# Scaling the attention probabilities on ScalarE, with one reciprocal and one gate product per pair of heads

## The chip, the cores and the metric

The kernel runs on one core of one Trainium2 chip. The metric is the device time of one launch in microseconds (us), as the median of several runs. The engines of the core are named as the profile names them: PE (TensorE matmul), PEld (TensorE weight load), DVE (VectorE), ACT (ScalarE), POOL (GpSimd) and SP (SyncE, which issues DMAs).

## The reference

Two layers, each on a residual stream of 512 positions by 1024 channels, all in float32:

```python
for l in range(DEPTH):                                   # DEPTH = 2
    x = x + 0.5 * swiglu_ffn(x, ffn1 ...)                # 1024 -> 2816 -> 1024
    h = rms_norm(x, mix_norm[l])
    p = h @ w_in[l]                                      # split into four groups
    y = concat[ pool_mixer(p_a), rwkv7_mixer(p_b), nsa_mixer(p_c), short_conv_mixer(p_d) ]
    x = x + y @ w_out[l]
    x = x + 0.5 * swiglu_ffn(x, ffn2 ...)
```

The change lies in the third mixer. Its four heads of 64 channels attend in three branches, and each branch's output is multiplied by a gate before the three are added:

```python
gt  = jax.nn.sigmoid(gates).reshape(B, S, H, 3)
out = gt[..., 0:1] * o_cmp + gt[..., 1:2] * o_sel + gt[..., 2:3] * o_win
# o_sel, o_win: softmax(q k^T * scale - slope * distance, causal) @ v
```

With 512 positions the selected and the window branch both reduce to full causal attention, each with keys and values of its own that all four heads share.

## The kernel before, in words

Every large product is made of three matmuls (`mm3`, lines 209 to 211): operands are cut into a high and a low part, so `hi*hi`, `lo*hi` and `hi*lo` are added in PSUM. The cut of a weight tile is a cast on ACT (line 203) and a subtraction on DVE (line 204).

A layer is a half-step FFN, the mixing stage, the output projection, and a second FFN. In the mixing stage the columns of the input projection arrive tile by tile (`tilep`), and four mixers work on them. Two of them are long chains of small operations that run side by side: the RWKV recurrence (`Rwkv.solve`, then `Rwkv.chain`, eight steps in two halves, each half followed by `Rwkv.out`), and the attention (`Net.nsa`).

The attention works through 16 units per layer: 4 query blocks `i` of 128 positions, 2 pairs of heads `j`, 2 branches `br`. For each unit, `scores(i, j, br)` computes the two heads of the pair, with `w = 128 * (i + 1)` keys:

- line 589, PE: two matmuls of queries and keys into a PSUM bank `d`;
- line 591, DVE: adds the distance bias, scales and writes the tile `s`, and leaves the row's extreme in `mx` (a short read of the accumulator follows);
- line 594, ACT: the exponential in place, with the row's sum in `sum` (again a short read of the accumulator follows);
- lines 596 and 597, DVE: the reciprocal of the sum, times the gate, in `cf`, one column per head;
- line 598, POOL: the tile `s` times `cf`, row by row.

`values` then transposes the probabilities of both heads on PE (line 616), cuts the result on ACT and DVE (lines 618 and 619), and multiplies by the values (line 623, with the compressed branch's line 627) into the PSUM bank `o`. After the second branch, lines 633 (ACT) and 634 (DVE) move the unit's output to `T`. When all units of a pair are done, `T` is cut for the output projection (lines 463 and 464).

The tiles `s` of scores and the cut transposes come out of one ring of seven buffers (`ring`, `rring`); `mx`, `sum` and `cf` have four buffers each.

What stands in which order on an engine is set by the framework's scheduler when the program is built, from the priorities in `Net.PRI` and its own costs: the recurrence has a better priority than the attention units, and these a better one than the remaining projection tiles, which fill in. Each engine then takes its instructions strictly in the order that was written down. Lines that come back in the prediction beside these: 904 and 911 or 912 (copies between the steps of the recurrence), 931 (its state update on DVE), 183 to 189 and 995 (normalisation in `Rwkv.out`), 216 (a scaled copy on ACT in the FFN), 355 (the reload of `x` after the mixers, issued from POOL).

Of the kernel before, what the change touches and what calls it, by code (L numbers as in the profile page):

```python
# [13 lines left out]
AF = mybir.ActivationFunctionType  # L14
ALU = mybir.AluOpType
# [83 lines left out]
class Net:  # L99
# [424 lines left out]
    def nsa(self, raw, L1, cmp):  # L524
        nc = self.nc
# [38 lines left out]
        gh = gt.rearrange("p (i h b) -> p i h b", h=4, b=3)  # L564
# [13 lines left out]
        def scores(i, j, br):  # L578
            w = P * (i + 1)
            out = []  # L580
            for hp in range(2):
                h = 2 * j + hp
                if hp == 0 or w > 256:
                    pq, sc, o = self.pd(), self.ring(), 0
                else:
                    o = w
                ph, sh = pq[:, o:o + w], sc[:, o:o + w]
                for k in range(2):
                    nc.tensor.matmul(ph, Q2[h][:, i * P:(i + 1) * P], K2[:, br, k, :w], start=(k == 0), stop=(k == 1))  # L589
                mx = self.small(1, "mx", bufs=4)  # L590
                nc.vector.tensor_tensor_reduce(sh, ph, c["bias"][:, S - w:S],
                                               -(2.0 ** (-2 * (h + 1))), 3.0e38, ALU.add, ALU.min, mx)
                sm = self.small(1, "sum", bufs=4)
                nc.scalar.activation(sh, sh, AF.Exp, bias=mx, scale=-1.0, accum_out=sm)
                cf = self.small(1, "cf", bufs=4)
                nc.vector.reciprocal(cf, sm)
                nc.vector.tensor_mul(cf, cf, gh[:, i, h, 1 + br:2 + br])
                nc.gpsimd.tensor_scalar(sh, sh, cf, None, ALU.mult)
                out.append(sh)
            return out  # L600

        def values(scs, i, j, br):
# [33 lines left out]
        def run():  # L636
            yt = self.mt("T16", [P, 2, S])
            self.y[4], self.y[5] = yt[:, 0], yt[:, 1]
            prev = None
            for u in units:  # L640
                sc = at(scores, *u)
                if prev is not None:
                    at(values, *prev)
                prev = (sc, *u)
                yield
            at(values, *prev)
# [578 lines left out]
```

## Time and profile before

| | |
|---|---|
| median of 3 runs | 2081.13 us (2078.3 to 2084.09) |
| the profiled execution | 2080.37 us, of which the profiled span is 2078.6 us |
| PE busy | 2026.1 us, 97% of the span |
| PEld busy | 1646.0 us, 79% |
| DVE busy | 1042.8 us, 50% |
| ACT busy | 665.3 us, 32% |
| POOL busy | 329.9 us, 16% |
| attention of layer 1, first to last line 589 | 521.8 to 627.8 us after the span's start |
| attention of layer 2, first to last line 589 | 1550.7 to 1650.1 us |

How to read it: busy time is the union of the records of an engine, and the records of overlapping matmuls run into each other, so a busy PE is not a PE at its peak. Shares over the whole span are an average over FFN stages, where PE works without a break, and mixing stages, where it waits for others. The change touches only the second kind.

### The profile page before, as it was taken

The page shows a single profiled execution, that of the slowest core. Times are in us where ns is not written, and L with a number is a line of the kernel's source. Part 1 is how long each engine was busy: PE and PEld are TensorE (multiplying, and loading weights), DVE is VectorE, ACT ScalarE, POOL GpSimd, SP SyncE. Part 2 cuts the span into 40 slices and gives each one's busy share as a digit, 9 for nine tenths or more (in the row PEclk, how much of TensorE's full clock was granted, in tenths as well). Part 3 has the DMA queues.
Part 4 walks back from the last instruction along what each step waited for, and adds up shares of the span by engine and source line. Part 5 has one row for each costly group of instructions (what it writes and reads, how often), then busy time and mean ns, then how long its engine had stood idle before and what let it go on. Part 6 is the DMA issues. An engine that isn't in the chain of part 4 may idle for free.

```text
span 2078.6 us, 25265 instructions
## 1 busy us (share of the span) xinstructions
PE 2026.1 (97%) x10132; PEld 1646.0 (79%) x10132; DVE 1042.8 (50%) x1866; ACT 665.3 (32%) x1053; POOL 329.9 (16%) x311
## 2 busy tenths in 40 slices
PE   8999999998999999999999999999988999999999
PEld 6888888876767888888888888887766778888887
DVE  5434344567676534343544343355686754334433
ACT  4322223332344322232333222233324443222221
POOL 1110111102332110011011001111033411100110
PEclk9999999998999999999999999999999999999999
DMA  5223223322302322322332232244133032223223
GB/s 198 93 90 103 101 89 124 128 102 64 71 18 91 102 89 82 114 90 89 104 102 102 84 110 100 75 133 149 68 74 77 1 102 102 95 84 116 86 92 97
DMA packets 61078, 196.76 MB, mean 95 GB/s; under 512 B 29472, under 2 KB 29600, under 8 KB 46240
## 3 DMA queue, kind: packets, MB, share of 16 engines
q1 hardware_dynamic: 58400, 186.76, 28.0%
q0 software_dynamic: 2560, 8.39, 1.1%
q8 instruction: 79, 1.29, 0.3%
q14 instruction: 39, 0.32, 0.0%
HBM read 183.58 MB, written 8.93 MB: 93 GB/s over the span
## 4 chain that ended last, share of the span: by engine, by line
PE 92%; DVE 4%; DMA 1%; issue 1%; ACT 1%; POOL 0%; SPq 0%; DVEq 0%; POOLq 0%; ACTq 0%
PE d L209 15%; PE d L210 15%; PE d L211 15%; PE r L211 8%; PE r L209 8%; PE r L210 8%; PE n L209 5%; PE n L211 5%; PE n L210 5%; PE o L623 1%; PE r L1010 1%; PE n L616 1%; PE d L589 0%; PE c L901 0%; DVE t L1032 0%
## 5 line engine op out<-in xcount | busy, mean ns | idle before, releaser
L203 ACT CAST wh<-w 128x1024 fp32r<-128x1024 f32 (+2 forms) x360 | 344.4, 957 | 1103.9 <-issue 334.5
L204 DVE TENSOR_TENSOR wl<-w,wh 128x1024 fp32r<-128x1024 f32 (+2 forms) x360 | 404.4, 1124 | 211.7 <-ACT wh L203 204.1
L209 PE MATMUL d<-hh,wh 128*128 128x512 f32 x1008 | 400.0, 397 | 6.8 <-ACT hh L216 6.8
L210 PE MATMUL d<-hl,wh 128*128 128x512 f32 x1008 | 400.6, 397 | 1.7 <-DVE hl L217 1.7
L211 PE MATMUL d<-hh,wl 128*128 128x512 f32 x1008 | 399.0, 396 | 0.0
L270 POOL TENSOR_TENSOR al<-t,ah 128x512 fp32r<-128x512 f32 x88 | 152.7, 1735 | 1062.5 <-ACT ah L269 1062.5
L210 PE MATMUL r<-hl,wh 128*128 128x512 f32 x736 | 286.8, 390 | 0.0
L211 PE MATMUL r<-hh,wl 128*128 128x512 f32 x736 | 286.5, 389 | 0.0
L209 PE MATMUL r<-hh,wh 128*128 128x512 f32 x736 | 286.5, 389 | 0.0
L209 PEld LDWEIGHTS d<-hh,wh 128*128 128x128 f32 x1008 | 192.6, 191 | 50.2 <-ACT hh L216 6.8
L210 PEld LDWEIGHTS d<-hl,wh 128*128 128x128 f32 x1008 | 192.4, 191 | 44.7 <-DVE hl L217 3.6
L211 PEld LDWEIGHTS d<-hh,wl 128*128 128x128 f32 x1008 | 192.4, 191 | 42.9 <-issue 2.0
L264 DVE TENSOR_TENSOR t<-d,rs 128x512 f32<-128x512 f32 x88 | 60.5, 691 | 266.3 <-PE d L211 260.5
L268 DVE TENSOR_TENSOR t<-t,r 128x512 f32<-128x512 f32 x88 | 60.5, 688 | 221.1 <-PE r L211 220.9
L209 PEld LDWEIGHTS r<-hh,wh 128*128 128x128 f32 x736 | 138.2, 188 | 28.7
L211 PEld LDWEIGHTS r<-hh,wl 128*128 128x128 f32 x736 | 138.2, 188 | 28.6
L210 PEld LDWEIGHTS r<-hl,wh 128*128 128x128 f32 x736 | 138.2, 188 | 28.5
L209 PE MATMUL d<-ah,wh 128*128 128x512 f32 x352 | 136.9, 389 | 0.0
L210 PE MATMUL d<-al,wh 128*128 128x512 f32 x352 | 136.9, 389 | 0.0
L211 PE MATMUL d<-ah,wl 128*128 128x512 f32 x352 | 136.9, 389 | 0.0
L209 PE MATMUL n<-ah,wh 128*128 128x512 f32 x352 | 136.9, 389 | 0.0
L210 PE MATMUL n<-al,wh 128*128 128x512 f32 x352 | 136.9, 389 | 0.0
(307 smaller groups left out, 2372.1 us busy)
## 6 DMA issues: line engine op xcount, KB each, us to landing
w<-in_g SPq DMA_DIRECT2D x87, 1024.0 KB, 4.9
w<-in_d SPq DMA_DIRECT2D x64, 704.0 KB, 4.1
w<-in_win SPq DMA_DIRECT2D x20, 1024.0 KB, 4.9
w<-in_wout SPq DMA_DIRECT2D x8, 1024.0 KB, 5.3
xd<-x POOLq DMA_DIRECT2D x16, 256.0 KB, 4.2
x<-xd POOLq DMA_DIRECT2D x16, 256.0 KB, 5.7
x<-in_x SPq DMA_DIRECT2D x8, 256.0 KB, 5.3
s<-in_cmpk SPq DMA_DIRECT2D x8, 256.0 KB, 5.9
```

The costliest lines, as they stand in the source:

```text
L203: self.nc.scalar.copy(hi, w)
L204: self.nc.vector.tensor_sub(lo, w, hi.bitcast(F32))
L209: self.nc.tensor.matmul(ps, wh[:, sl], xh[:, k], start=(first and i == 0), stop=False)
L210: self.nc.tensor.matmul(ps, wh[:, sl], xl[:, k], start=False, stop=False)
L211: self.nc.tensor.matmul(ps, wl[:, sl], xh[:, k], start=False, stop=(last and i == n - 1))
L264: nc.vector.tensor_mul(t, pg, self.rs)
L268: nc.vector.tensor_mul(th, th, pu)
L270: nc.gpsimd.tensor_sub(al, th, ah.bitcast(F32))
L616: nc.tensor.transpose(ptr[:, k * P:(k + 1) * P], scs[hp][:, b * P:(b + 1) * P], self.ident)
L623: nc.tensor.matmul(acc, VT[:, br, b], pT[k][:, o:o + 2 * P], start=(br == 0 and b == 0 and k == 0), stop=(br == 1 and b == i and k == 1))
L1010: nc.tensor.matmul(pm[:, i * P:(i + 1) * P], AK[j][hs, ch].rearrange("p a b -> p (a b)"), KR[j][hs, ch].rearrange("p a b -> p (a b)"), sta ...
```

## The change

The two heads of a unit now share one `sum` tile and one `cf` tile of two columns. The exponential of each head writes its sum into its own column. After both heads, one reciprocal and one product with the gates (two gates, strided) serve the pair, and two ACT instructions multiply the two score tiles by their column of `cf`. POOL no longer takes part in the attention units.

```diff
         def scores(i, j, br):
             w = P * (i + 1)
             out = []
+            sm = self.small(2, "sum", bufs=4)
             for hp in range(2):
...
-                sm = self.small(1, "sum", bufs=4)
-                nc.scalar.activation(sh, sh, AF.Exp, bias=mx, scale=-1.0, accum_out=sm)
-                cf = self.small(1, "cf", bufs=4)
-                nc.vector.reciprocal(cf, sm)
-                nc.vector.tensor_mul(cf, cf, gh[:, i, h, 1 + br:2 + br])
-                nc.gpsimd.tensor_scalar(sh, sh, cf, None, ALU.mult)
+                nc.scalar.activation(sh, sh, AF.Exp, bias=mx, scale=-1.0, accum_out=sm[:, hp:hp + 1])
                 out.append(sh)
+            cf = self.small(2, "cf", bufs=4)
+            nc.vector.reciprocal(cf, sm)
+            nc.vector.tensor_mul(cf, cf, gh[:, i, 2 * j:2 * j + 2, 1 + br])
+            for hp in range(2):
+                nc.scalar.activation(out[hp], out[hp], AF.Copy, scale=cf[:, hp:hp + 1])
             return out
```

In the changed program the exponential is still line 594, the reciprocal is line 597, the product line 598 and the scaling line 600; every later line is one higher. The scheduler wrote both mixing stages anew.

**First place: ACT, layer 1, the first two units with 512 keys.** Here `s` is a score tile, `n` a bank of transposes, `R` and `sav` belong to the recurrence, `T` takes a unit's output. Before:

```order
L594 ACTIVATE s_4513,sum_4518<-s_4513,mx_4516 128x512
L463 CAST yh_4240<-t_4910 128x256 x2
L594 ACTIVATE s_4525,sum_4530<-s_4525,mx_4528 128x512
L618 CAST s_4541<-n_4536 128x512
L911 COPY sav_2608<-c_4982 64x128
L618 CAST s_4552<-n_4549 128x256
L594 ACTIVATE s_4563,sum_4568<-s_4563,mx_4566 128x512
L633 COPY T_619_3930<-o_4487 64x128
L594 ACTIVATE s_4575,sum_4580<-s_4575,mx_4578 128x512
```

And in the changed program:

```order
L594 ACTIVATE s_4466,sum_4464<-s_4466,mx_4469 128x512
L619 CAST s_4489<-n_4484 128x512
L594 ACTIVATE s_4473,sum_4464<-s_4473,mx_4476 128x512
L619 CAST s_4500<-n_4497 128x256
L905 COPY R_4916<-c_4909 128x128
L634 COPY T_619_3930<-o_4439 64x128
L594 ACTIVATE s_4512,sum_4510<-s_4512,mx_4515 128x512
L594 ACTIVATE s_4519,sum_4510<-s_4519,mx_4522 128x512
L600 ACTIVATE s_4466<-s_4466,cf_4479 128x512
L600 ACTIVATE s_4473<-s_4473,cf_4479 128x512
L912 COPY sav_2608<-c_4918 64x128
L634 COPY T_619_3930<-o_4439 64x128
```

The two scalings of a unit stand behind the two exponentials of the unit after it, and a copy of the recurrence (line 912 there) stands behind the scalings.

**Second place: DVE, the coefficients of the same stretch.** Before, with four instructions for the unit's two heads:

```order
L596 RECIPROCAL cf_4570<-sum_4568 128x1
L634 TENSOR_TENSOR T_619_3930<-T_619_3930,o_4487 64x128
L596 RECIPROCAL cf_4582<-sum_4580 128x1
L597 TENSOR_TENSOR cf_4570<-cf_4570,gt_3376 128x1
L597 TENSOR_TENSOR cf_4582<-cf_4582,gt_3376 128x1
```

And in the changed program, with two for the pair:

```order
L598 TENSOR_TENSOR cf_4479<-cf_4479,gt_3376 128x2
L189 SCALAR_TENSOR_TENSOR lrs_4824<-ru_861_4827,lrs_4824 128x8
L635 TENSOR_TENSOR T_619_3930<-T_619_3930,o_4439 64x128
L996 TENSOR_TENSOR t_4812<-t_4812,lrs_4824 128x512
L597 RECIPROCAL cf_4525<-sum_4510 128x2
L598 TENSOR_TENSOR cf_4525<-cf_4525,gt_3376 128x2
L913 COPY sav_2608<-c_4918 64x128
```

The pair's reciprocal and product each appear once, and they now come after the second head's sum.

## Rows read from the trace of the kernel before

**Rows 1.** The page's first part: span, then each engine's busy time, its share of the span and its instructions.

```profile
span 2078.6 us, 25265 instructions
PE 2026.1 (97%) x10132; PEld 1646.0 (79%) x10132; DVE 1042.8 (50%) x1866; ACT 665.3 (32%) x1053; POOL 329.9 (16%) x311
```

**Rows 2.** Busy time by stretch of the mixing stages: the stretch in us from the span's start, its length, then busy us and instructions of PE, PEld, DVE, ACT and POOL, the granted TensorE clock, DMA share and GB/s. The first two lie in layer 1, the third in layer 2.

```profile
560.00:600.00 40.00, 36.63 (x270) 27.00 (x270) 24.95 (x89) 18.68 (x53) 10.83 (x11) 0.88 0.08 27
600.00:640.00 40.00, 38.71 (x294) 29.35 (x293) 33.04 (x121) 20.77 (x55) 17.30 (x12) 0.98 0.01 1
...
1590.00:1640.00 50.00, 47.04 (x405) 34.86 (x399) 36.42 (x132) 26.43 (x76) 18.39 (x16) 0.97 0.07 23
```

**Rows 3.** Timeline of POOL in layer 1's mixing stage: start and duration in us, engine, line, operation, operands, and in brackets the idle time before it and what ended it. A row with x2 holds two scalings back to back.

```profile
552.43 0.61 POOL L598 TENSOR_SCALAR s<-s,cf 128x128 f32<-128x128 f32 x1 [11.05 <-DVE cf L597]
...
565.77 0.93 POOL L598 TENSOR_SCALAR s<-s,cf 128x256 f32<-128x256 f32 x1 [7.66 <-DVE cf L597]
...
587.61 2.47 POOL L598 TENSOR_SCALAR s<-s,cf 128x384 f32<-128x384 f32 x2 [0.45 <-DVE cf L596]
596.77 1.24 POOL L598 TENSOR_SCALAR s<-s,cf 128x384 f32<-128x384 f32 x1 [6.70 <-DVE cf L596]
...
615.25 3.37 POOL L598 TENSOR_SCALAR s<-s,cf 128x512 f32<-128x512 f32 x2 [3.31 <-DVE cf L597]
621.34 3.10 POOL L598 TENSOR_SCALAR s<-s,cf 128x512 f32<-128x512 f32 x2 [2.73 <-DVE cf L597]
627.22 3.11 POOL L598 TENSOR_SCALAR s<-s,cf 128x512 f32<-128x512 f32 x2 [2.77 <-DVE cf L597]
633.22 3.11 POOL L598 TENSOR_SCALAR s<-s,cf 128x512 f32<-128x512 f32 x2 [2.90 <-ACT s L594]
648.56 3.86 POOL L355 DMA_DIRECT2D x<-xd  x7 [12.23 <-DVE yl L464]
```

**Rows 4.** Groups of ACT over the whole span, by line and shape: count, then busy us and mean ns of one, then idle time before them and what ended most of it.

```profile
L216 ACT ACTIVATE hh<-x,vec 128x512 fp32r<-128x512 f32 x48 | 34.5, 719 | 35.8 <-DVE x L309 33.7 <-DVE x L363 2.2
...
L618 ACT CAST s<-n 128x512 fp32r<-128x512 f32 x32 | 18.3, 585 | 22.5 <-PE n L616 22.3
...
L594 ACT ACTIVATION_READ_ACCUMULATOR s<-s,mx 128x1 f32 x64 | 12.0, 188 | 0.0
...
L594 ACT ACTIVATE s<-s,mx 128x512 f32<-128x512 f32 x16 | 11.6, 723 | 8.7 <-DVE mx L591 6.1 <-DVE cf L596 1.9 <-DVE cf L597 0.6
...
L594 ACT ACTIVATE s<-s,mx 128x384 f32<-128x384 f32 x16 | 9.8, 615 | 5.4 <-DVE lrs L184 2.6 <-DVE mx L591 2.3 <-DVE cf L596 0.5
...
L594 ACT ACTIVATE s<-s,mx 128x256 f32<-128x256 f32 x16 | 8.1, 509 | 6.1 <-DVE cf L597 2.9 <-DVE mx L591 2.5 <-ACT s L618 0.4
...
L594 ACT ACTIVATE s<-s,mx 128x128 f32<-128x128 f32 x16 | 6.4, 402 | 21.7 <-DVE mx L591 17.9 <-DVE cf L596 3.8
```

**Rows 5.** Timeline of ACT for one unit with 512 keys in layer 1, columns as in rows 3.

```profile
624.39 0.72 ACT L594 ACTIVATE s<-s,mx 128x512 f32<-128x512 f32 x1
625.02 0.19 ACT L594 ACTIVATION_READ_ACCUMULATOR s<-s,mx 128x1 f32 x1
626.13 0.72 ACT L594 ACTIVATE s<-s,mx 128x512 f32<-128x512 f32 x1 [0.92 <-DVE cf L596]
626.76 0.18 ACT L594 ACTIVATION_READ_ACCUMULATOR s<-s,mx 128x1 f32 x1
```

**Rows 6.** Groups of DVE over the whole span, columns as in rows 4.

```profile
L597 DVE TENSOR_TENSOR cf<-cf,gt 128x1 f32<-128x1 f32 x64 | 11.7, 186 | 1.3
...
L596 DVE RECIPROCAL cf<-sum 128x1 f32<-128x1 f32 x64 | 10.1, 158 | 9.1 <-ACT s L594 8.6
```

**Rows 7.** Two groups of DVE in the stretch 1590 to 1672 us (layer 2), columns as in rows 4.

```profile
L995 DVE TENSOR_TENSOR t<-t,lrs 128x512 f32<-128x512 f32 x2 | 1.4, 699 | 0.0
...
L188 DVE TENSOR_TENSOR ru<-ru,rh 128x8 f32<-128x8 f32 x6 | 1.0, 162 | 0.1
```

**Rows 8.** The chain of work that ended last, in the stretch 560 to 648 us: shares of the chain by engine and line.

```profile
by line: PE o L623 13.0%; PE n L616 7.2%; PE d L589 5.8%; PE c L901 5.4%; PE o L627 5.0%; DVE s L591 5.0%; PE c L898 4.7%; PE r L948 4.2%; issue 3.8%; DVE yl L464 3.4%; PE r L951 3.1%; ACT s L618 2.7%; DVE T L634 2.6%; PE r L969 2.4%; PE c 
```

**Rows 9.** The group of line 591 on DVE in the stretch 560 to 646 us, columns as in rows 4; and its accumulator read.

```profile
L591 DVE CUSTOM_DVE_ANT_0 s<-d,cst 128x384 f32<-128x384 f32 (+2 forms) x22 | 12.2, 564 | 2.0 <-PE o L623 1.9
...
L591 DVE DVE_READ_ACCUMULATOR2_ANT mx<- 128x1 f32 x22 | 1.8, 82 | 0.0
```

**Rows 10.** The same two groups in the stretch 560 to 648 us (layer 1).

```profile
L995 DVE TENSOR_TENSOR t<-t,lrs 128x512 f32<-128x512 f32 x2 | 1.6, 825 | 0.1
...
L188 DVE TENSOR_TENSOR ru<-ru,rh 128x8 f32<-128x8 f32 x6 | 1.4, 238 | 0.1
```

**Rows 11.** Timeline of DVE, the coefficients of the unit in rows 5.

```profile
625.95 0.16 DVE L596 RECIPROCAL cf<-sum 128x1 f32<-128x1 f32 x1
...
626.87 0.15 DVE L597 TENSOR_TENSOR cf<-cf,gt 128x1 f32<-128x1 f32 x1
...
627.91 0.15 DVE L596 RECIPROCAL cf<-sum 128x1 f32<-128x1 f32 x1
...
628.11 0.15 DVE L597 TENSOR_TENSOR cf<-cf,gt 128x1 f32<-128x1 f32 x1
```

## Prediction

> **What bounds the kernel now.** I read the page first, then the mixing stages by stretch, then one attention unit engine by engine, and last the chain of work that ended last. The page has PE busy for 97% of the span [rows 1], so at first sight nothing that spares VectorE or GpSimd can count. The stretches tell it otherwise. In the 40 us from 600 us on, deep in layer 1's attention, PE is busy for 38.71 us, but its weight loads for only 29.35, while VectorE is busy for 33.04 of 40 us, ScalarE for 20.77 and GpSimd for 17.30 [rows 2]. No engine is full there and all wait for each other in turn. The POOL timeline shows the pace: the pairs of scalings with 512 keys start at 615.25, 621.34, 627.22 and 633.22 us, one unit each 6.0 us [rows 3]. The stage is a loop of short dependent steps, with VectorE the fullest after PE.
>
> How much of PE's 38.71 us is real decides what can be won at all. The record of a matmul reaches past the start of the next, so the gaps of a loop are partly covered by the tail of the matmul ahead; the weight loads, one for each matmul, leave 10.65 us of these 40 free [rows 2]. If the busy figure were the truth, 1.3 us could be won here. The Trainium skill, "Perfetto Trace Analysis", section "Identifying the Most-Contended Engine", calls matmul busy time a bad metric, since matmuls are pipelined, and wants the busy share of weight loads instead; by that rule up to 10.65 us of the stretch are open, by the busy row 1.3.
>
> The executions shown: the profiled one took 2080.37 us (span 2078.6), the median of the runs is 2081.13, 0.8 above it. I make the sum as a difference and set it against the median.
>
> **The change part by part, for one layer (16 units); there are two layers.**
>
> *Scaling moves from POOL to ACT: the latency of a unit.* On POOL one scaling takes 0.61, 0.93, 1.24 and 1.57 us for 128, 256, 384 and 512 keys (half of 3.11 for the last), and two heads go one behind the other: 3.11 us for 512, 2.47 for 384 [rows 3]. On ACT the trace has no such row at SBUF-to-SBUF with a column as scale for all widths; the nearest are the exponential with a column as bias, 0.40, 0.51, 0.62 and 0.72 us, and the FFN's scaled copy at 512, 0.72, which agrees [rows 4]. Two in a row overlap by about 0.1 us: the exponential starts at 624.39, and its accumulator read at 625.02, before its 0.72 us are over [rows 5]. So a pair takes 1.34 us at 512, 1.13 at 384, 0.92 at 256 and 0.70 at 128. But the pair must wait for the second head's sum, which comes later than the first by one exponential and its 0.19 us read, less the overlap of 0.1: 0.8, 0.7, 0.6 and 0.5 us.
> - Upper bound, where POOL does both heads back to back: 3.11 - (0.8 + 1.34) = 0.97 at 512; 2.47 - (0.7 + 1.13) = 0.64; 1.86 - (0.6 + 0.92) = 0.34; 1.22 - (0.5 + 0.70) = 0.02. Four units each: 7.9 us.
> - Lower bound, where the second head is late enough for POOL to be free: 1.57 - 1.34 = 0.23; 1.24 - 1.13 = 0.11; 0.93 - 0.92 = 0.01; 0.61 - 0.70 = -0.09. Four each: 1.0 us.
>
> All four 512 pairs of layer 1 are back to back, 384 partly [rows 3], so I take four times 0.97, two times 0.64 and two times 0.11 at 384, and 0.3 for the rest: 5.7 us. Not all of it ends up in the time, for the next unit's scores run meanwhile and VectorE is 83% busy. I count half: **2.8 us**.
>
> *VectorE's small instructions.* Four become two per unit. One reciprocal (0.158 us) and one product (0.186) fewer [rows 6], 16 times: 5.5 us of VectorE. Two columns instead of one should cost the same: line 188's eight columns take 0.162 us [rows 7]. Of line 591, which stands in the same queue at the same places, 5.0% of an 88 us chain [rows 8] = 4.4 us lie on the chain, of 12.2 + 1.8 = 14.0 us busy [rows 9]: 31%. The same share of 5.5 us: **1.7 us**; between 0 and 5.5.
>
> *VectorE next to POOL.* Some small VectorE rows are stretched in layer 1 where scalings run: line 188 takes 0.238 us in place of 0.162, six times, and line 995 takes 0.825 in place of 0.699, twice [rows 7, 10], together 0.7 us; such rows stand in the recurrence's normalisation. They should fall back. I count half: **0.3 us**. The Trainium skill, "SBUF — State Buffer", section "Who interferes with whom", says that a VectorE instruction with two SBUF inputs and a GpSimd instruction that reads SBUF exclude each other, the later one waiting for the whole of the first; by that a stretch could be 1.5 us, and the term would be some twice as large, but the rows show a mean stretch of 0.08 to 0.13 us.
>
> *ScalarE gets fuller.* Eight scalings of each width, 8 x (0.40 + 0.51 + 0.62 + 0.72) = 18.0 us, less 0.1 for each of 32: 14.8 us. Its share in the 40 us stretch goes from 52% to about 70%. The casts of line 618 and the copies of the recurrence stand in the same queue, behind scalings that wait for coefficients. Nothing to some 5 us of it can surface; ScalarE was idle for 19 of the 40 us [rows 2], and its casts mostly waited for PE (22.3 of 22.5 us) [rows 4], so I take a tenth: **-1.5 us**.
>
> *Rest.* POOL's freed time is worth nothing by itself: the reload of `x` that stands behind the last scaling in its queue waited 12.23 us, for something else [rows 3]. The shared `sum` and `cf` tiles are written and read at the same points as before, four of each; no DMA is added and none is moved past another on SP.
>
> Sum: 2.8 + 1.7 + 0.3 - 1.5 = 3.3 us per layer, 6.6 in both; the tail of each stage ends with a 512 unit whose 0.97 us lie bare, of which half is counted above, so I add 0.2 per layer. 2081.1 - 7.0 = **2074.1 us**.
>
> **The rivals.**
>
> *Nothing that can be measured.* PE takes its instructions in a fixed order with projection tiles between the units, and what the units gain is lost in waits elsewhere in the loop, or the new order of both stages costs as much as the relief brings. For it: PE's 97%, and that POOL does not appear among the lines of the chain [rows 8], so its latency may be hidden as it is. Against it: the 6.0 us pace with 3.1 us of POOL in it. By the terms, with a quarter of what I expect, 1.8 us: 2079.3 us. A measurement of this kernel can tell about 0.3%, 6 us, from no change.
>
> *Twice as much.* If the pace of the loop is the unit's own latency, the whole 5.7 to 7.9 us per layer come through, with VectorE's 1.7 on top: 7.4 to 9.6 per layer, 2062 to 2066 us, say 2064. For it: back-to-back pairs at a constant pace; against it: VectorE at 83%.
>
> *Slower: ScalarE's queue.* The scaling is now an instruction at the head of an in-order queue, waiting for two VectorE instructions. In the unit at 624 us the second sum was there at 626.94 (626.76 + 0.18), the product only at 628.26 [rows 5, 11]: 1.3 us; for the first head it took from 625.2 to 627.0, 1.8 us. If ScalarE stands still for 1.5 us in each of the 11 units of the dense part, with casts and the recurrence's copies behind it, that is 16.5 us per layer; a third of it bare is 5.5, less VectorE's 1.7: 3.8 per layer, 2081.1 + 7.6 = 2088.7 us. It decides where ScalarE's idle time before line 600 passes about 12 us per layer and PE waits for line 618's casts behind it. Against it: the scheduler put two exponentials of the next unit ahead of most scalings, so the wait is mostly filled. The Trainium skill, "ScalarE: Activation LUTs", section "Rules for kernel authors", sends multiplications to VectorE and not to ScalarE; by that rule this case is the likelier one, but no row here shows the scaling on VectorE.
>
> **How the numbers follow.** The forecast (2066 to 2075) gets 0.40, the larger gain 0.12, no measurable change 0.34, slower 0.14. Faster by over 0.3% is the first two: 0.52. The range leaves out about a tenth at either end: 2062 us, where the larger gain is nearly whole, to 2087, within the slower case.
>
> **What would show it.** Right: line 598's POOL rows are gone; the ACT group of line 600 has means of 0.40 to 0.72 us; the reciprocal and the product count 32 each instead of 64, at about 0.16 us; the last unit's pace at 512 keys falls from 6.0 to about 5.4 us; the distance from the first score matmul of a layer to the first unbroken run of output-projection matmuls shrinks by 3 to 4 us; line 188 goes to 0.16 us in both layers. Wrong, if the pace stays at 6 us with VectorE less busy (then the loop hangs on something else, PE or the recurrence), or if ACT waits long before line 600 and PE before line 623 for the casts.

## The result, and the profile after

The changed kernel took 2058.7 us (median of 4 runs, 2053.1 to 2059.4), the kernel before beside it 2081.8: a ratio of 0.9889, 95% interval 0.9866 to 0.9913. A second measurement gave 2058.6 and 0.9898 (0.9880 to 0.9917). So 23 us were won where 7 were forecast, and the time lies 3 us below the low end of the range.

The page's first part, which answers to [rows 1]:

```profile
span 2057.7 us, 25078 instructions
...
PE 2012.5 (98%) x10132; PEld 1636.9 (80%) x10132; DVE 1031.3 (50%) x1802; ACT 693.5 (34%) x1117; POOL 256.4 (12%) x247
```

The same kind of groups as in [rows 4, 6, 7], on ACT and DVE in 560 to 632 us (layer 1); line 600 is the scaling, lines 597 and 598 are the pair's coefficients, and line 188 has kept its number:

```profile
L594 ACT ACTIVATE s<-s,mx 128x512 f32<-128x512 f32 x8 | 5.8, 723 | 0.2 <-DVE lrs L189 0.2
L600 ACT ACTIVATE s<-s,cf 128x512 f32<-128x512 f32 x8 | 5.3, 714 | 0.3 <-DVE cf L598 0.3
...
L600 ACT ACTIVATE s<-s,cf 128x384 f32<-128x384 f32 x8 | 4.4, 603 | 0.0
```

```profile
L597 DVE RECIPROCAL cf<-sum 128x2 f32<-128x2 f32 x11 | 1.8, 163 | 1.7 <-ACT s L594 1.5
...
L598 DVE TENSOR_TENSOR cf<-cf,gt 128x2 f32<-128x2 f32 x11 | 1.7, 158 | 0.2
...
L188 DVE TENSOR_TENSOR ru<-ru,rh 128x8 f32<-128x8 f32 x6 | 1.0, 162 | 0.1
```

Every duration came out as forecast: scalings at 0.60 and 0.71 us, a reciprocal of two columns at 0.16, and line 188 back at 0.162. That isn't where 23 us come from. The pace of the 512-key units, which was to fall from 6.0 to 5.4 us [rows 3], did not: the last two pairs of scalings start 5.95 us apart, and from the first pair's start to the fourth's it is 18.4 us, before 18.0. The timeline of ACT, line 600, 512 keys, in layer 1 (start and duration in us):

```profile
605.02 1.32 ACT L600 ACTIVATE s<-s,cf 128x512 f32<-128x512 f32 x2
606.80 1.33 ACT L600 ACTIVATE s<-s,cf 128x512 f32<-128x512 f32 x2
617.44 1.34 ACT L600 ACTIVATE s<-s,cf 128x512 f32<-128x512 f32 x2 [0.29 <-DVE cf L598]
623.39 1.34 ACT L600 ACTIVATE s<-s,cf 128x512 f32<-128x512 f32 x2
```

What did change is seen when each layer's mixing is cut at two events that exist in every kernel: the **solve part** runs from the first score matmul to the last matmul of the recurrence's solve (line 1085 before, 1086 after), the **rest** to the last matmul of attention and recurrence. Busy time by stretch (columns as in [rows 2]), before: layer 1's two parts, then layer 2's:

```profile
521.80:552.90 31.10, 28.29 (x407) 22.69 (x407) 20.48 (x62) 11.51 (x31) 10.80 (x11) 0.95 0.52 111
552.90:644.80 91.90, 86.30 (x619) 65.09 (x611) 64.92 (x229) 42.55 (x117) 32.00 (x27) 0.91 0.06 18
1550.90:1594.20 43.30, 37.13 (x446) 29.44 (x446) 26.56 (x90) 15.54 (x43) 14.93 (x18) 0.92 0.38 80
1594.20:1672.90 78.70, 73.21 (x579) 54.71 (x572) 57.88 (x202) 38.56 (x105) 26.99 (x21) 0.98 0.04 15
```

And after:

```profile
522.50:554.10 31.60, 29.73 (x418) 23.64 (x416) 20.92 (x62) 15.15 (x43) 4.74 (x3) 0.95 0.49 110
554.10:633.20 79.10, 75.83 (x605) 58.42 (x599) 57.23 (x195) 52.36 (x136) 1.30 (x1) 1.00 0.04 15
1540.40:1572.20 31.80, 29.59 (x414) 23.54 (x414) 21.28 (x64) 15.16 (x43) 4.74 (x3) 0.95 0.48 110
1572.20:1651.40 79.20, 75.92 (x611) 58.50 (x605) 57.40 (x195) 52.37 (x137) 1.29 (x1) 1.00 0.04 15
```

The mixing falls from 245.0 to 221.7 us: 12.8 in layer 1's rest, 11.5 in layer 2's solve. After, both layers take the same time; before, each had a weak spot of its own. The granted clock is the second thing to see: 0.91 in the slow rest of layer 1, 1.00 after. The weight loads show it too, since their number hardly differs (sums over the four stretches): 171.9 us for 2036 of them before, 164.1 for 2034 after.

Both spots lie in stages that the scheduler wrote anew, and the question for the experiments is how much of the 23 us is order, and how much the work itself.

### The profile page after: what moved, and what is told of

Same layout as the page of the kernel before. It is cut to its first block, busy times and chain, and to the rows that moved or that the text cites. A ratio compares the mean times of both kernels' runs of the same rounds, so it can differ in the third digit from the quotient of the medians.

```text
span 2057.7 us, 25078 instructions
## 1 busy us (share of the span) xinstructions
PE 2012.5 (98%) x10132; PEld 1636.9 (80%) x10132; DVE 1031.3 (50%) x1802; ACT 693.5 (34%) x1117; POOL 256.4 (12%) x247
## 4 chain that ended last, share of the span: by engine, by line
PE 93%; DVE 3%; ACT 1%; DMA 1%; issue 1%; POOL 0%; SPq 0%; DVEq 0%
PE d L210 16%; PE d L209 16%; PE d L211 16%; PE r L211 8%; PE r L210 8%; PE r L209 8%; PE n L209 5%; PE n L211 5%; PE n L210 5%; PE o L624 1%; PE r L1011 1%; PE n L617 1%; PE d L590 1%; PE c L902 1%; DVE t L1033 0%
## 5 line engine op out<-in xcount | busy, mean ns | idle before, releaser
L211 PE MATMUL n<-ah,wl 128*128 128x512 f32 x352 | 137.0, 389 | 0.0
```

What stands on the lines that cost most here:

```text
L211: self.nc.tensor.matmul(ps, wl[:, sl], xh[:, k], start=False, stop=(last and i == n - 1))
```

## The experiments

Two theories. **Order**: the change made the scheduler write other orders, and these carry the gain. **Work**: the shorter scaling on ACT and the fewer DVE instructions carry it. Twelve runs follow, in three groups. A kernel in another's order gets lists of instructions and a function that adds dependencies for the scheduler alone, without waits:

```diff
         tile_hybrid_trunk(tc, *args, out)
+        impose(tc, nc)
...
+    for chain in ORDER:
+        for a, b in zip(chain, chain[1:]):
+            tc.add_manual_dep(found[f"I-{b}"], f"I-{a}", info, reason="order")
```

Writing an order down costs nothing by itself that shows: the run further below that has before's order with one SP row moved takes 31.2 and 91.8 us for the two parts of layer 1, before 31.1 and 91.9.

**Half of the change at a time.** The paired coefficients with the scaling left on POOL:

```diff
-                nc.scalar.activation(out[hp], out[hp], AF.Copy, scale=cf[:, hp:hp + 1])
+                nc.gpsimd.tensor_scalar(out[hp], out[hp], cf[:, hp:hp + 1], None, ALU.mult)
```

> The changed kernel with the scaling left on POOL; sum, reciprocal and gate product for the pair as changed. Theory E (engine: a pair of scalings takes 3.1 us on POOL and 1.4 on ACT at 512 keys, and this is the gain): 2074 to 2081 us, little of the 23 us. Theory D (VectorE: half as many small instructions is the gain): 2058 to 2064. Theory O (the scheduler happened on a better order): anywhere between, not tied to either part.

2080.8 us, ratio 1.0003 (0.9992 to 1.0014). The other half, ScalarE with a reciprocal and a product for each head:

```diff
-                nc.gpsimd.tensor_scalar(sh, sh, cf, None, ALU.mult)
+                nc.scalar.activation(sh, sh, AF.Copy, scale=cf)
```

> The kernel before with the scaling alone moved to ACT, one reciprocal and one product per head as before. E: 2059 to 2066 us, most of the gain. D: 2077 to 2082. If both parts are needed (the pairing keeps VectorE's queue short while ACT waits for it): 2068 to 2074.

2081.3 us, 1.0000 (0.9989 to 1.0012). Neither half moves the time, and both together win 23 us: parts that add up would not do that. The second half's mixing took 116.5 us in layer 1, better than before's 123.0, and 135.9 in layer 2, worse than 122.0 (the stage ahead of the first score is 7.4 us shorter there in turn, 107.7 against 115.1). Then the changed work with the scaling on VectorE:

```diff
-                nc.scalar.activation(out[hp], out[hp], AF.Copy, scale=cf[:, hp:hp + 1])
+                nc.vector.tensor_scalar(out[hp], out[hp], cf[:, hp:hp + 1], None, ALU.mult)
```

> The changed kernel with the scaling on VectorE in place of ACT (paired coefficients). E, read as latency of the scaling alone: 2058 to 2066, if VectorE scales 512 keys in under 0.7 us. If VectorE's fill is what sets the pace (82% busy in the densest 40 us before): 32 scalings more per layer cost more than the pairing spares, 2068 to 2085.

2068.0 us, 0.9938 (0.9923 to 0.9953), in an order of its own. It puts 26.5 us of scalings (64, on average 0.42 to 0.48 us by width) on the queue that the forecast called the fullest, and still beats before by 12 us. Since work and order both changed, it credits neither.

**The order held fixed.** The first half's work (paired, POOL) in the changed kernel's order:

> Scaling on POOL with paired coefficients, as in the first of these runs, but PE, VectorE and ACT take their instructions in exactly the order of the changed kernel (the order is imposed). E: the order does not help, 2074 us or more, and PE waits for the scalings; slower than the first run by up to 10 us, since this order was written for another engine. O: 2057 to 2063, as the changed kernel, since the order is the gain.

2069.6 us, 0.9952 (0.9931 to 0.9972), between the two theories; in its trace SP and POOL keep the changed kernel's order too. The work of before, untouched, in that order:

> The work of the kernel before (scaling on POOL, one reciprocal and one product for each head), with the five engines in the order of the changed kernel; a pair's two reciprocals and two products stand where the one of each stands there. The paired work on POOL in this order took 2069.6 us (0.995 of before). If the order alone carries that gain and VectorE's 32 + 32 small instructions are hidden: 2067 to 2073 us. If VectorE's count matters once the order is good, they bring back up to 2 x 5.5 us: 2076 to 2081. Rival, if the order itself is worth nothing and pairing was needed: 2080.

2069.4 us, 0.9953 (0.9938 to 0.9967). **The order alone is worth about 10 us** (10.6 by the medians; the interval of the ratio spans 7 to 13), with every instruction of before in it. The medians of the two runs agree to 0.2 us, so pairing is worth nothing there that shows; the intervals leave room for a few us. Its stretches, layer 1 and layer 2:

```profile
517.50:549.80 32.30, 28.02 (x418) 22.41 (x416) 22.37 (x73) 12.95 (x35) 9.92 (x13) 1.00 0.48 107
549.80:632.30 82.50, 77.38 (x607) 58.45 (x600) 60.39 (x219) 40.17 (x112) 31.57 (x25) 1.00 0.04 14
1541.50:1575.20 33.70, 29.66 (x418) 23.61 (x416) 22.40 (x73) 12.99 (x35) 9.94 (x13) 0.95 0.43 103
1575.20:1657.80 82.60, 77.48 (x608) 58.42 (x602) 60.48 (x219) 40.28 (x112) 31.57 (x25) 1.00 0.04 14
```

In this execution (2067.1 us) the mixing is 231.1 us, 13.9 less than before. Both weak spots are gone, while layer 2's rest is 3.9 us longer. The weight loads' own time fell by 9.0 us (162.9 against 171.9), which is the clock; what share of the 13.9 us that makes isn't shown, since loads overlap matmuls. The second half's work (ScalarE, unpaired) in that order:

> Scaling on ScalarE, but one reciprocal and one product for each head (as in the run of ScalarE alone, which took 2081.3 us in its own order), with all five engines in the order of the changed kernel; a unit's two reciprocals and products stand where the one of each stands there. If pairing is worth nothing once the order is the changed kernel's, as it was with POOL (2069.4 and 2069.6): 2057 to 2061 us. If VectorE's count matters where ScalarE scales: 2062 to 2069.

2059.8 us, 0.9903 (0.9879 to 0.9926). So in this order **ScalarE in POOL's place is worth about 10 us** (9.6 by the medians, 10.4 by the ratios), and pairing again nothing that shows: the changed kernel itself, run beside it, took 2058.6.

> The changed kernel again, unedited, beside the other three on one chip, to set them against: 2055 to 2061 us by every theory. Its stages tell how far one execution differs from the next: 119.6 and 115.5 us from a layer's first matmul of the mixing to the first score in the two layers of the run shown.

Where most of these 10 us sat, PE's waits show. Work of before in the new order, layer 1's rest (us in total, times, longest):

```profile
PE n L616 <- POOL s L598: 3.0, 5, 0.9
PE o L623 <- ACT s L618: 0.6, 2, 0.4
```

The kernel before, the same stage:

```profile
PE c L898 <- DVE H L931: 1.3, 1, 1.3
PE c L910 <- DVE TT L1088: 1.0, 1, 1.0
PE d L589 <- DVE mx L591: 0.9, 1, 0.9
```

In before's order PE waits for POOL for 0.3 us in both layers together; it waits for the recurrence and the solve. In the new order's rest these three waits are gone, and most of what is left is for POOL's scalings: 3.6 us over both parts of layer 1, 4.1 in layer 2. In the changed kernel PE waits for no scaling, and the rests shrink from 82.5 and 82.6 to 79.1 and 79.2. ScalarE's fuller queue takes something back: in each layer PE waits for line 965 on ACT, which stands behind two pairs of scalings, and with POOL in the same order that wait isn't there. The changed kernel, layer 1's rest:

```profile
PE r L949 <- ACT t L965: 1.2, 1, 1.2
```

That raises the counter-question: the changed work in an order in which PE waits for POOL for 0.7 us in all, that of the first half's kernel (paired, POOL).

> The work of the changed kernel (paired, scaling on ScalarE) with PE, VectorE, POOL and SP, and the rest of ScalarE, in the order that the scheduler wrote for the paired work on POOL (which took 2080.8 us, 1.000 of before). In the order of the changed kernel, ScalarE in POOL's place was worth 11 us (2069.6 against 2058.7). If the shorter scaling is worth as much in any order: about 2069 us. If it counts only where the order lets PE use it: 2077 to 2081. If scalings in this order block ScalarE's queue: over 2083.

2087.9 us, 1.0037 (1.0024 to 1.0050): slower than before, by 7.8 us. So the shorter scaling isn't worth the same in any order; in this one it costs. The changed work in before's own order was not run. The rests of an execution of 2092.6 us, layers 1 and 2:

```profile
550.90:645.90 95.00, 86.30 (x617) 64.19 (x611) 61.35 (x204) 55.32 (x143) 1.26 (x1) 0.93 0.05 17
...
1599.80:1684.20 84.40, 77.53 (x581) 58.56 (x574) 53.99 (x181) 48.62 (x124) 0.00 (x0) 0.92 0.04 14
```

PE waits there for casts behind ACT and DVE (lines 619 and 620: 1.9 and 2.3 us in layer 1) and for the recurrence's state (line 932: 3.3 us in layer 2). Which scaling holds up which of them was not taken apart.

**What in the order.** Two pieces were tried by themselves. The first is one row on SP. In layer 2, before issues the first 1 MB load of the output projection between the write of the solve's 16x16 inverses and their reload; the changed kernel issues it behind. Before:

```profile
1554.42 1.36 SPq L1037 DMA_DIRECT2D tdram<-t  x2
1556.08 0.91 SPq L193 DMA_DIRECT2D w<-in_wout  x1
1557.51 1.34 SPq L1042 DMA_DIRECT2D T<-tdram  x2
```

Moving that row behind the reloads in before, all else in before's order:

```diff
 L1037 DMA tdram<-t 128x16x16 x2
-L193 DMA w<-in_wout 128x2048
 L1042 DMA T<-tdram 64x16x64 x2
 L1042 DMA TT<-tdram 64x16x64 x2
+L193 DMA w<-in_wout 128x2048
```

> The kernel before, all five engines in their own order, but for one row: in layer 2 the first 1 MB load of the output projection stands on SP behind the reloads of the inverses in place of ahead of them, as in the changed kernel. Reloads in layer 2 landed after 7.3 us with the load ahead, after 4.5 without it (changed kernel), and the last matmul of the solve came at 158.4 us after the layer's start against 147.4. If the load is what holds layer 2's solve: it ends some 3 to 8 us earlier and the time falls to 2072 to 2077 us. If the solve's lateness is due to VectorE's and POOL's order: 2079 to 2081, with the reload shorter and the wait moved.

2077.9 us, 0.9991 (0.9981 to 1.0001): some 2 us, with nothing and 4 us both inside the interval. The opposite move in the changed kernel:

> The changed kernel, all engines in their own order, but for one row: in layer 2 the first 1 MB load of the output projection stands on SP ahead of the reloads of the inverses, as in the kernel before. If that load is a cause by itself: the reloads land after about 7 us in place of 4.5, and the time rises by 3 to 8 us, to 2062 to 2067 (against 2058.7). If it is hidden in this order: 2057 to 2060.

2065.6 us, 0.9920 (0.9906 to 0.9934), worse than the changed kernel by 7 us by the medians and by 5 to 6 by the ratios. Its solve part in layer 2, against 31.80 us at 0.95 without the move, and what PE waits for there (the execution shown took 2060.8 us, since layer 1's stage ahead of the scores took 115.6 us in it, in place of 119.6):

```profile
1534.70:1572.70 38.00, 33.58 (x418) 26.88 (x416) 21.09 (x64) 15.24 (x43) 4.73 (x3) 0.82 0.44 92
```

```profile
PE r L1058 <- DMA T<-tdram: 2.6, 2, 1.7
```

The reload (KB each, median us to landing), first in the changed kernel, then with the load ahead of it:

```profile
T<-tdram SPq DMA_DIRECT2D x2, 256.0 KB, 4.5
T<-tdram SPq DMA_DIRECT2D x2, 256.0 KB, 7.2
```

It lands 2.7 us later, as in before (7.3), PE waits 2.6 us and the clock falls to 0.82. So the row costs 5 to 7 us where the solve is what PE waits for, and hardly anything in before, where VectorE holds the solve back as well: with the row moved, the reload took 4.5 us, and the solve part still 42.8 us, with PE waiting for VectorE's lines 1067 (2.2 us), 619 (1.1), 782 (0.9) and 591 (0.8). Two causes stood side by side; taking one away shows little. The second half's kernel has two such loads ahead, and giving it the changed kernel's SP order did not help it either:

> The run of ScalarE alone (unpaired, 2081.3 us in its own order), all engines in that order but SP, which has the changed kernel's: in layer 2 the two 1 MB loads of the output projection stand behind the solve's transfers in place of ahead of them, and two smaller rows trade places. In its own order layer 2's mixing took 135.9 us against 116.5 in layer 1. If the loads are the cause: layer 2 falls to 116 to 124 us and the time to 2067 to 2073. If layer 2's lateness comes from the other engines' order: 2078 to 2081.

2085.7 us, 1.0014 (1.0000 to 1.0028), outside both. Layer 2's solve part grew from 51.3 to 59.8 us. What ACT, DVE and PE wait for in it:

```profile
ACT wh L203 <- DMA w<-in_wout: 4.0, 1, 4.0
DVE wl L204 <- ACT wh L203: 4.2, 1, 4.2
PE d L589 <- DVE mx L591: 8.6, 3, 4.1
```

In that order the cut of the loaded tile (lines 203 and 204) stands ahead of scores, so the load that was moved behind is now waited for itself, and line 591 behind it; PE waited 3.1 us for line 591 before the move. So this run doesn't tell what the loads cost ahead of the reloads. In that kernel's own order PE waits for no reload, so the loads are not what is seen to hold its solve.

The second piece is the clock in layer 1's rest. This is how PE's rows stand at the end of layer 1's solve, before (rows of a kind put together, buffer numbers left out):

```
 L1077 MATMUL r<-T,M x16
 L1077 MATMUL r<-T,M x16
 L1085 MATMUL r<-TT,T x16
 L589 MATMUL d<-K,kr x4
 L1085 MATMUL r<-TT,T x16
 L910 MATMUL c<-R,TT
```

and in the changed kernel, whose transposes and value products stand between the steps:

```
 L1078 MATMUL r<-T,M x16
 L617 MATMUL n<-cst,s
 L607 MATMUL n<-cst,KS
 L1078 MATMUL r<-T,M x16
 L617 MATMUL n<-cst,s
 L590 MATMUL d<-K,kr x4
 L1086 MATMUL r<-TT,T x16
 L624 MATMUL o<-s,VT
 L628 MATMUL o<-pct,vc x2
 L624 MATMUL o<-s,VT
 L1086 MATMUL r<-TT,T x16
 L911 MATMUL c<-R,TT
```

The trace of before in steps of 2 us (the clock is the third figure from the end) shows what follows such waits:

```profile
552.00:554.00 2.00, 1.10 (x36) 0.86 (x35) 1.47 (x5) 1.43 (x6) 0.96 (x2) 0.90 0.03 8
554.00:556.00 2.00, 1.94 (x9) 1.74 (x9) 1.88 (x9) 0.12 (x1) 1.51 (x2) 0.50 0.00 0
556.00:558.00 2.00, 2.00 (x8) 1.43 (x7) 1.21 (x5) 0.95 (x3) 1.74 (x2) 0.50 0.00 0
...
572.00:574.00 2.00, 0.76 (x9) 0.55 (x6) 1.91 (x8) 0.72 (x3) 0.00 (x0) 1.00 0.88 373
574.00:576.00 2.00, 2.00 (x15) 1.28 (x14) 1.83 (x10) 0.40 (x2) 1.53 (x2) 0.52 0.00 0
576.00:578.00 2.00, 2.00 (x9) 1.64 (x9) 0.22 (x2) 0.00 (x0) 1.19 (x2) 0.50 0.00 0
...
594.00:596.00 2.00, 0.68 (x13) 0.54 (x14) 1.89 (x8) 1.27 (x5) 0.00 (x0) 1.00 0.00 0
```

Twice PE is short of work for about a microsecond, and then the clock stands at half (0.50, that is 1.2 of 2.4 GHz) until about 560 and 581 us, and a third time from 598 to 601, after a wait at 594. The run of before with the SP row moved, whose layer 1 is before's, has all three at the same places, so they are no accident of one execution. PE reads as busy in the rows shown at 0.50, for 1.94 to 2.00 of 2.00 us, though only 8 or 9 matmuls stand in each. To test whether idle time is the cause, two matmuls with an overwritten result were put into before, which is more work and nothing else:

```diff
             pa = net.psum("c", 1)
+            if ch < 2 and not hasattr(net, "filled"):
+                nc.tensor.matmul(pa, net.c["bd"], net.c["bias"], start=True, stop=True)
```

> The kernel before, all engines in its own order, with two matmuls of 128x512 fp32 added in layer 1 whose results are overwritten: one where PE waits 1.1 us for the solve's last sum (line 910, chunk 0, 552.9 us), one ahead of line 910 of chunk 1 (571.6 us), 1.1 us before PE waits 1.1 us for a score tile. In before, the granted clock stands at 0.5 from 553.8 to 561.8 and from 574 to 581.5 us, just behind these waits. If PE's idle time there is what lowers the clock: one or both stretches come out at 1.00 and layer 1 is shorter by 3 to 8 us, 2072 to 2077 us. If the clock falls for another reason: the stretches stay, and the time is the same or up to 2 us longer, 2080 to 2082.

2075.1 us, 0.9980 (0.9965 to 0.9995): faster, though the added matmuls take 3.1 us of PE's time. The stretch after the second one:

```profile
572.00:574.00 2.00, 1.62 (x15) 0.79 (x14) 1.91 (x8) 0.64 (x3) 0.00 (x0) 1.00 0.89 377
574.00:576.00 2.00, 2.00 (x20) 1.38 (x20) 1.83 (x9) 0.48 (x2) 1.46 (x2) 1.00 0.01 4
576.00:578.00 2.00, 2.00 (x16) 1.51 (x16) 0.74 (x3) 0.59 (x1) 1.27 (x2) 1.00 0.00 0
```

The second and the third stretch at half clock are gone; the first stayed (0.64 and 0.50 in 552 to 556 us). Layer 1's rest fell from 91.9 to 88.3 us:

```profile
552.90:641.20 88.30, 84.03 (x619) 62.08 (x615) 64.74 (x228) 42.38 (x117) 31.85 (x27) 0.96 0.05 19
```

At the second place PE's idle time (two waits, 1.2 us together) is what let the clock fall, and the drop cost more than the idle time itself: some 7 us at half speed, an estimate of up to 3.4 us lost. At the first place that isn't shown: the added matmul took 2.1 us there and 1.0 at the second place, so the clock was down before it could help. The third stretch went without a matmul of its own, and why isn't shown; a wait that leaves PE 0.90 us of work in 2 us, at 592 us, did not lower the clock in this run.

## Why the prediction was wrong

The direction was right, the size wrong by a factor of three, and what the sum left out was the largest term.

- **The step that failed is "Rest" and what stands behind it: that the new order is neutral.** The sum costed instructions and took the scheduler's order as given, with "the new order of both stages" only as a loss in a rival. Measured with before's own work, it is worth about 10 us. The text also says that no DMA is moved past another on SP; one was, in layer 2, and putting it back costs the changed kernel 5 to 7 us.
- **The evidence was in the rows quoted.** The first stretch of [rows 2] has a granted clock of 0.88 and 36.63 us of PE in 40; the argument was built on the second, at 0.98. The same 40 us after hold 330 matmuls in place of 270, at 1.00 (the row below). A lower clock inside a stage of dependent steps was a loss that an order could give back, and the prediction never priced it.

```profile
560.00:600.00 40.00, 38.76 (x330) 28.96 (x330) 31.24 (x110) 29.90 (x81) 0.00 (x0) 1.00 0.08 28
```

- **Scaling's latency** (2.8 us per layer counted, 0.2 for the tail, bounds 1.0 to 7.9): the size was near, the condition missing. In the new order it is some 4.7 us per layer (231.1 to 221.7 over both), 3.4 of them in each rest. In the two other orders in which ScalarE scaled, the gain didn't show (2081.3) or turned into a loss (2087.9), and PE waited for others there; for before, [rows 8] hinted at it: POOL isn't on that chain.
- **VectorE's small instructions** (1.7 us per layer): nothing that shows, in two pairs of runs at one order (2069.6 and 2069.4 on POOL, 2058.6 and 2059.8 on ACT). A share of the chain was taken for a price.
- **VectorE next to POOL** (0.3 us): line 188 did go from 0.238 [rows 10] to 0.162 us. The Trainium skill, "SBUF — State Buffer", section "Who interferes with whom", has the two engines exclude each other; the trace agrees only in part. The stretched rows vanish with POOL's scalings, but so they do in the work of before in the new order, where POOL still scales (rows below, whole span). There a row of line 995 stands inside four scalings that take 6.94 us, where two take 3.11. No run shows what the term is worth; it is bounded by the rows' 0.7 us.

```profile
L188 DVE TENSOR_TENSOR ru<-ru,rh 128x8 f32<-128x8 f32 x24 | 3.9, 163 | 0.6
...
L995 DVE TENSOR_TENSOR t<-t,lrs 128x512 f32<-128x512 f32 x4 | 2.7, 686 | 0.1
```

- **ScalarE fuller** (-1.5 us per layer): line 600 waited 6.4 us in all; in layer 1's rest PE waited 0.8 us for casts, 0.6 with POOL in the same order, and 1.2 us for line 965 behind the scalings. The size was near, and the 4.7 us above are net of it.
- **The slower rival** (2088.7 us) is what the changed work does in the order of the first half's kernel: 2087.9. Its price fits; its own sign, line 600 waiting over 12 us per layer, does not (7.2 us in both layers together), so its mechanism isn't shown and the match may be luck.
- **Wrong by its own signs**: the pace at 512 keys stayed at 6 us, while VectorE's work in layer 1's rest fell from 64.9 to 57.2 us, which the text named as the sign that the loop hangs on something else. The distance from the first score to the end of the mixing shrank by 12.3 and 11.0 us, not by 3 to 4. The Trainium skill, "Perfetto Trace Analysis", section "Identifying the Most-Contended Engine", says that the busy share of matmuls is no good measure of how close a kernel is to the roofline, and the trace agrees: PE went from 97% to 98% busy while 1% of the time disappeared.

What stays open: why this work in particular led the scheduler to the better order, which of the other engines' rows hold back layer 2's solve in before, how much of the order's gain is clock and how much waits, and why the clock falls ahead of the first added matmul.

## What to carry to other kernels

Where a scheduler writes the order, an edit has two effects, the work and the new order, and they don't add: try each half, and the old work in the new order, before crediting either. Look at the granted clock by stretch inside stages of dependent steps, since a microsecond without work there was followed by several at half speed, while PE still read as busy. And compare the DMA queue row by row: a large load ahead of a small transfer on which a solve waits was worth 5 to 7 us here, where nothing else held the solve, and some 2 us or nothing where something did.

## What the runs showed of the hardware

- PE's clock fell to half after waits of 0.9 to 1.3 us among small matmuls (busy 0.68 to 1.10 us of 2 us), and yet not after every such wait: in the changed kernel, a wait of 1.2 us at 608 us (columns as above) left it at full speed.

```profile
608.00:610.00 2.00, 0.91 (x17) 0.91 (x19) 1.92 (x7) 2.00 (x5) 0.00 (x0) 1.00 0.00 0
```

- The stage ahead of the first score, with its 568 or 569 matmuls, takes 119.6 us at a mean clock of 0.93 or 115.5 at 0.97, even in the two layers of one execution, here of the changed kernel. Single executions of one kernel differ by such steps of 4 us, so times 4 us apart need many runs.

```profile
402.90:522.50 119.60, 111.94 (x568) 85.94 (x568) 85.55 (x182) 39.46 (x68) 20.27 (x32) 0.93 0.29 89
1424.90:1540.40 115.50, 108.08 (x569) 82.97 (x569) 85.38 (x179) 39.29 (x68) 21.18 (x32) 0.97 0.30 92
```
